# Scores of 64-feature heads over all 128 rows, keys padded with zero halves

## The chip, the cores and the metric

The kernel runs on 1 core of one Trainium2 chip. The metric is the device time of an execution in microseconds (us), as the median of several runs. On the engines' names: TensorE (PE in the rows, with PEld for its weight loads) multiplies matrices, VectorE (DVE) and ScalarE (ACT) work elementwise, POOL (GpSimd) and SP (SyncE) mostly issue transfers and small fills. TensorE multiplies a stationary operand of K rows by up to 128 columns with a moving operand of K rows by N columns; the rows are contracted.

## The reference

256 tokens of 1024 features go through two blocks. The first has FFNs, a pool mixer and multi-head latent attention (MLA) with 16 heads; the second an even layer (forgetting attention and sliding-window attention, 8 heads each, then an FFN) and an odd layer (sparse attention of 16 heads over the 64 best keys that an indexer of 8 heads picks, then a mixture of 8 experts). Cut to the scores:

```python
# MLA: 128 + 64 features
s = einsum('bqhd,bkhd->bhqk', qn_b, k_nope) + einsum('bqhr,bkr->bhqk', qr_b, k_rope)
# even layer: 64 features a head
s = einsum('bqhd,bkhd->bhqk', qi, k) * scale + ci[..., :, None] - cum[..., None, :]   # 8 forgetting heads
s = einsum('bnqhgd,bnshd->bnhgqs', qb, kk) * D ** -0.5                                # 8 window heads, with sinks
# odd layer
logits = einsum('bqhd,bsd->bqhs', iqi, ik)                     # indexer, 8 heads of 64
score = einsum('bqh,bqhs->bqs', iwi, relu(logits))
_, idx = top_k(score, 64)
s = einsum('bqhgd,bqthd->bhgqt', qi, ks) * scale               # 16 heads of 64, over the chosen keys
```

Each is followed by a mask, a softmax over the keys and a product with the values.

## The kernel before

Tokens stand on partitions in two blocks of 128 (`tb`) for the residual stream; operands of a product are transposed, features on partitions. Every float32 operand of a large product is split into a high and a low float32r part: `split` (L157) has ScalarE write the high part (L161, with a factor L164) and VectorE the rest (L162, L166). A product is then three passes, `mm3`, on lines 170, 171 and 172.

`attention` (L745) is a loop over heads, software-pipelined: in turn i it makes the scores of head i and their softmax (`soft`), transposes the weights of head i-2 and splits them (`turn`), and multiplies those of head i-3 with the values (`value`); at the end of a group of heads `project` multiplies with the output weights. In `soft`, the score products fill half of a PSUM tile `psa` per token block; VectorE adds the mask and takes the maximum (L760), ScalarE the exponential with its sum (L764), VectorE one reciprocal for each head (L770), and ScalarE and VectorE one half of the scaling each (L774, L776).

Scores of 64-feature heads use half of the rows: two heads share a tile of 128 partitions, and `score64` (L1002) takes the slice of 64 rows from 0 or from 64 of both operands, `xh` and `xl`, over 256 keys. The MLA's score has a product over 128 rows (`kq`, named `ah`, `al` in the rows) and one over 64, the rotated part, with the shared key `krT` (L986 to 994). `forget` (L1087) adds two products over 64 rows with one column of the constant `sel`. The indexer of the odd layer (L1174) uses `score64` too, eight heads that alternate between the two halves of the rows; its keys lie in a part of `KK`, the tile of the sparse attention's keys.

Operand pairs of 1024 columns come from `xpair`, five buffers. The order of the instructions on each engine is set when the kernel is built: a tile scheduler places them by priority as written and inserts the semaphores; at run time each engine takes its list in order. Loads of one row to all partitions (`brow`, L545) are issued by POOL. Rows of the profile that carry the names `psacc` are products of `project` or of an FFN.

Of the kernel before, what the change touches and what calls it, by code (L numbers as in the profile page):

```python
# [21 lines left out]
P = 128  # L22
# [17 lines left out]
# columns of the constant array  # L40
# [3 lines left out]
def host_consts():  # L44
    """Arrays that depend on shapes alone."""
# [19 lines left out]
    for r in range(8):  # L65
        hc[r::32, C_SEL + r] = 1
# [12 lines left out]
class Net:  # L79
# [49 lines left out]
    def wsplit(self, raw, n):  # L129
        """Splits n <= 1024 columns."""  # L130
        H, L = (self.wp.tile([P, 1024], F32R, tag=t, name=self.nm(t), bufs=6) for t in ("wh", "wl"))
        with self.issued_after(self.hold):
            self.split(H[:, :n], L[:, :n], raw)
        return H[:, :n], L[:, :n]

    def issued_after(self, ins):
        """The work of ins's engine in the block comes after it."""
        return self.tc.issue_after(ins.ins) if ins else nullcontext()

    def wunits(self, w, rows, c0, n, fine=False):  # L140
        """Row blocks of w[:, c0:c0+n], [128, n] each, as a list over k of (H, L)."""
# [15 lines left out]
    def split(self, H, L, src, scale=None):  # L157
        """H + L = src * scale."""
# [20 lines left out]
    def squares(self, x, n, add, scale=1.0):  # L179
        """The sum of (scale * x)^2 over the n features of x [128, n] + add -> [128, 1]."""  # L180
# [13 lines left out]
    def rsqrt(self, v, n):  # L194
        """(v / n)^-1/2: the bits of v give a start, Newton's method the rest."""
# [25 lines left out]
    class XT:  # L221
        """A [1024 features, 256 tokens] operand in two pairs of tiles [128, 4, 256]."""
# [15 lines left out]
    def to_T(self, x, tb, X, g):  # L238
        """X[:, tb] = (x * g)^T."""
# [17 lines left out]
    def xtile(self, tb):  # L257
        return self.xp.tile([P, D], F32, tag=("xh", "xl")[tb], name=self.nm("xn"), bufs=5)

    def normed(self, tb):  # L260
        """rmsnorm without gain."""
# [5 lines left out]
    def normed_twice(self, tb):  # L267
        """h = rmsnorm(h) * gain, then rmsnorm of that without gain."""
# [6 lines left out]
        # with a the mean square of h, b that of t = h * gain: h' = t (a + eps)^-1/2,  # L275
        # h' (b / (a + eps) + eps)^-1/2 = t (b + eps (a + eps))^-1/2
# [6 lines left out]
    def to_T_mod(self, x, tb, X, g, sh):  # L283
        """X[:, tb] = (x * g + sh)^T."""
# [9 lines left out]
    def lin(self, X, w, c0, n, ws=None, feed=None):  # L294
        """Yields (tb, psum) = X^T w[:, c0:c0+n], tokens on partitions; feed(tb) makes X[:, tb]."""
# [14 lines left out]
    def lin_T(self, X, w, c0, n, Q, scale):  # L310
        """Q[H, L] [128, n/128 * 256] = (X^T w[:, c0:c0+n] * scale)^T."""
        for g in range(0, n, 256):
# [7 lines left out]
            self.split(Q[0][:, a:a + 512], Q[1][:, a:a + 512], o, scale)  # L320

    def residual(self, tb, acc, factor, last=True):
        """h[tb] += acc * factor, acc two halves [128, 512]."""
# [6 lines left out]
    def gated_residual(self, tb, acc, g):  # L330
        """h[tb] += acc * g, g [128, 1024] the same on every partition."""
# [19 lines left out]
    def swiglu(self, jobs, hook=None, ws0=None, feed=None):  # L351
        """jobs: (x(k, tb), token blocks, rstd() or None, wg, wu, wd, F, done(tb, acc), which may
        return more to do later); gate and up of a chunk of hidden columns run ahead of the transposes and the down
        product of the one before."""
# [11 lines left out]
        def gate_up(i, up):  # L366
# [3 lines left out]
            # the first chunk takes its token blocks one after the other, as they come  # L370
# [61 lines left out]
        # the last two chunks finish one token block after the other  # L432
# [42 lines left out]
    def then(extra, hook):  # L475
        """A hook that makes one more call in each of its first turns."""
# [16 lines left out]
    def rows(self, rows, vecs):  # L493
        """Vectors of features as rows of 128."""
# [7 lines left out]
    def columns(self, rows, r, at):  # L502
        """The rows as columns."""
# [17 lines left out]
    def constants_late(self):  # L521
# [6 lines left out]
        # rows t' of block b against all tokens: 1 where t' <= token  # L528
# [21 lines left out]
    def ada_plan(self, layer):  # L550
# [21 lines left out]
        def turn(m, acc):  # L572
            """The sum over partitions of acc, as columns."""
# [43 lines left out]
    def gate_rows(self, layer, m):  # L617
        """The gate vector of 1024 features on every partition."""
# [27 lines left out]
        # weights times the scale of their column and the gain of their row  # L646
# [11 lines left out]
        # the first token block needs nothing of the second  # L658
# [26 lines left out]
    def rope(self, src, tab, nh, out):  # L685
        """src, out [128, nh, 64]; tab = (cos, sin) [128, 64] each, both halves alike."""
# [10 lines left out]
    def rope_tables(self):  # L697
        """cos, sin of positions * inv_freq for the second block."""
        nc = self.nc
        pi = self.small(2, I32)  # L700
        nc.gpsimd.dma_start(pi, rowmajor(self.A["positions_2"], (1, P), (P, 2)))
# [4 lines left out]
        # 2 pi in parts whose multiples are exact  # L706
# [26 lines left out]
    def pairs_T(self, x, tb, blocks, Q, base, scale=None):  # L733
        """Q columns base + j*256 + tb*128 = transposed 128-column blocks of x."""
# [3 lines left out]
        H, L = (q[:, base:base + m * S].rearrange("p (j t) -> p j t", j=m)[:, :, tb * P:(tb + 1) * P] for q in Q)  # L738
        self.split(H, L, t[:, :m * P].rearrange("p (j t) -> p j t", j=m), scale)

# [1 line left out]
    # columns of the scores that the queries of a token block can see: [block 0: 128 keys, unused | block 1: 256 keys]  # L742
# [761 lines left out]
```

## Time and profile before

| what | value |
|---|---|
| runs, median (lowest to highest) | 1896.49 us (1894.69 to 1899.66), 3 runs |
| profiled execution, first to last instruction (span) | 1894.1 us; the profile gives no other time for it; the median is 2.4 us above |
| busy: TensorE, VectorE, ScalarE, POOL | 1830.5, 1418.2, 1082.2, 7.0 us |
| mean granted TensorE clock | 0.956 |
| chain that ended last | TensorE 88%, VectorE 7%, ScalarE 3%, DMA 2% |

Reading it: busy time is from the first to the last moment of instructions of an engine, and shares over the whole span mix stages with different limits. The granted clock is the share of TensorE's full speed that the chip lets through; 1.00 is 2.4 GHz and 0.50 is 1.2 GHz. A busy TensorE at 0.50 does half as much.

### The profile page before, as it was taken

How to read it: one execution, taken by the hardware profiler on the slowest of the kernel's cores; microseconds unless marked ns; L12 is line 12 of the kernel's file. 1: busy time of each engine (PE TensorE's matmuls, PEld its weight loads, DVE VectorE, ACT ScalarE, POOL GpSimd, SP SyncE). 2: the span in 40 equal slices, each digit the busy share in tenths (PEclk: the TensorE clock that was granted, in tenths of full speed). 3: DMA queues.
4: the chain of work that ended last, by engine and by line, in shares of the span. 5: the costliest groups of instructions: out<-in, count | busy, mean ns of one | idle time of the engine just before them, and what ended most of it. 6: DMA issues, size and time to landing. Idle time of an engine off the chain costs nothing.

```text
span 1894.1 us, 24484 instructions
## 1 busy us (share of the span) xinstructions
PE 1830.5 (97%) x9045; PEld 1563.8 (83%) x9045; DVE 1418.2 (75%) x2516; ACT 1082.2 (57%) x1704; POOL 7.0 (0%) x21
## 2 busy tenths in 40 slices
PE   8999999999999999999999999999898999999996
PEld 6889788988888888888888878898677888888885
DVE  6668976688767777876775465458936899999997
ACT  6444644465445656544565454356444888777875
POOL 0000000000000000000000000000000000000000
PEclk9999999999999999999997799999858999999998
DMA  8758677767766134776652145555304699999993
GB/s 306 246 195 318 219 278 250 240 222 260 262 216 234 55 123 160 260 259 213 222 167 88 45 137 195 161 190 167 103 15 145 244 337 333 334 331 341 334 359 142
DMA packets 179446, 412.40 MB, mean 218 GB/s; under 512 B 7203, under 2 KB 57574, under 8 KB 179190
## 3 DMA queue, kind: packets, MB, share of 16 engines
q1 hardware_dynamic: 178694, 409.12, 62.4%
q0 software_dynamic: 592, 1.62, 0.3%
q8 instruction: 73, 1.20, 0.3%
q14 instruction: 55, 0.45, 0.1%
q10 hardware_dynamic: 32, 0.01, 0.0%
HBM read 409.67 MB, written 1.05 MB: 217 GB/s over the span
## 4 chain that ended last, share of the span: by engine, by line
PE 88%; DVE 7%; ACT 3%; DMA 2%; issue 1%; SPq 0%; POOL 0%; ACTq 0%; DVEq 0%
PE psa L170 18%; PE psa L171 17%; PE psa L172 17%; PE psacc L170 8%; PE psacc L172 8%; PE psacc L171 8%; PE pstr L236 4%; DVE wl L162 2%; ACT wh L161 1%; PE pstr L171 1%; PE pstr L170 1%; PE psa L1326 1%; PE pstr L172 1%; ACT aa L187 1%; PE pstr L1357 1%
## 5 line engine op out<-in xcount | busy, mean ns | idle before, releaser
L162 DVE TENSOR_TENSOR wl<-raw,wh 128x1024 fp32r<-128x1024 f32 (+2 forms) x720 | 817.2, 1158 | 279.7 <-ACT wh L161 273.5
L161 ACT ACTIVATE wh<-raw 128x1024 fp32r<-128x1024 f32 (+2 forms) x720 | 712.5, 1008 | 514.4 <-PE psa L172 273.9
L170 PE MATMUL psa<-wh,xh 128*128 128x512 f32 (+3 forms) x1536 | 570.2, 372 | 18.4 <-ACT xh L161 11.5
L171 PE MATMUL psa<-wl,xh 128*128 128x512 f32 (+3 forms) x1536 | 564.9, 368 | 3.0 <-DVE wl L162 2.9
L172 PE MATMUL psa<-wh,xl 128*128 128x512 f32 (+3 forms) x1536 | 562.7, 368 | 0.0
L170 PEld LDWEIGHTS psa<-wh,xh 128*128 128x128 f32 x1536 | 290.6, 189 | 60.6 <-ACT xh L161 12.5
L171 PEld LDWEIGHTS psa<-wl,xh 128*128 128x128 f32 x1536 | 290.9, 189 | 42.4 <-DVE wl L162 6.2
L172 PEld LDWEIGHTS psa<-wh,xl 128*128 128x128 f32 x1536 | 290.1, 189 | 37.4 <-DVE xl L166 0.5
L170 PE MATMUL psacc<-wh,ah 128*128 128x512 f32 x616 | 239.7, 393 | 1.5 <-ACT wh L161 1.5
L171 PE MATMUL psacc<-wl,ah 128*128 128x512 f32 x616 | 240.5, 390 | 0.2
L172 PE MATMUL psacc<-wh,al 128*128 128x512 f32 x616 | 240.5, 390 | 0.0
L170 PEld LDWEIGHTS psacc<-wh,ah 128*128 128x128 f32 x616 | 115.6, 188 | 25.1 <-ACT wh L161 2.3
L171 PEld LDWEIGHTS psacc<-wl,ah 128*128 128x128 f32 x616 | 115.8, 188 | 24.3 <-DVE wl L162 1.1
L172 PEld LDWEIGHTS psacc<-wh,al 128*128 128x128 f32 x616 | 115.7, 188 | 24.2
L568 DVE SCALAR_TENSOR_TENSOR big<-raw,csil,big 128x1024 f32<-128x1024 f32 x84 | 107.7, 1282 | 2.7 <-DMA raw<-in_e_ada_w 1.7
L236 PE MATMUL pstr<-ident,aa 128*128 128x128 f32 x432 | 70.5, 293 | 6.5 <-DVE aa L695 5.2
L162 DVE TENSOR_TENSOR al<-pstr,ah 128x512 fp32r<-128x512 f32 (+2 forms) x86 | 52.4, 634 | 29.9 <-ACT ah L161 29.4
L236 PEld LDWEIGHTS pstr<-ident,aa 128*128 128x128 f32 x432 | 54.5, 149 | 17.5 <-issue 3.1
L161 ACT ACTIVATE ah<-pstr 128x512 fp32r<-128x512 f32 (+2 forms) x86 | 44.7, 553 | 25.2 <-PE pstr L236 20.3
L170 PE MATMUL psacc<-wh,xh 128*128 128x512 f32 (+1 forms) x144 | 54.8, 386 | 0.1
L171 PE MATMUL psacc<-wl,xh 128*128 128x512 f32 (+1 forms) x144 | 54.6, 379 | 0.0
L172 PE MATMUL psacc<-wh,xl 128*128 128x512 f32 (+1 forms) x144 | 54.6, 379 | 0.0
(309 smaller groups left out, 1925.3 us busy)
## 6 DMA issues: line engine op xcount, KB each, us to landing
raw<-in_o_exp_down SPq DMA_DIRECT2D x40, 1024.0 KB, 6.7
raw<-in_o_exp_gate SPq DMA_DIRECT2D x32, 1024.0 KB, 8.7
raw<-in_o_exp_up SPq DMA_DIRECT2D x32, 1024.0 KB, 9.7
raw<-in_e_ada_w SPq DMA_DIRECT2D x24, 1024.0 KB, 6.8
raw<-in_o_ada_w SPq DMA_DIRECT2D x24, 1024.0 KB, 5.4
raw<-in_ffn_pre_wd SPq DMA_DIRECT2D x20, 1024.0 KB, 6.4
raw<-in_ffn_post_wd SPq DMA_DIRECT2D x20, 1024.0 KB, 6.3
raw<-in_ffn_pre_wu SPq DMA_DIRECT2D x16, 1024.0 KB, 5.7
```

What stands on the lines that cost most here:

```text
L161: nc.scalar.activation(H, src, AF.Copy)
L162: nc.vector.tensor_sub(L, src, H.bitcast(F32))
L170: mm(out, x[0], w[0], start=start, stop=False)
L171: mm(out, x[0], w[1], start=False, stop=False)
L172: mm(out, x[1], w[0], start=False, stop=stop)
L187: nc.scalar.activation(junk[:, c], x[:, c], AF.Square, scale=scale, accum_out=ss[:, i:i + 1])
L236: self.nc.tensor.transpose(out[:, j * P:(j + 1) * P], src[:, b * P:(b + 1) * P], self.ident)
L568: nc.vector.scalar_tensor_tensor(acc, src, self.csil[:, k:k + 1], acc, op0=ALU.mult, op1=ALU.add)
L1326: nc.tensor.matmul(o[:, j * S:(j + 1) * S], XN[tb][part][:, (k + j) * P:(k + j + 1) * P], sel[tb], start=n == 0, stop=n == 3)
L1357: nc.tensor.matmul(t, selT[e][:, tb * P:(tb + 1) * P], y[hf][part], start=part == 0, stop=part == 1)
```

## The change

Keys of the 64-feature heads get 128 rows: each head pair's keys are written twice as wide, into two blocks of 256 columns, of which the first has keys on rows 0 to 63 and zeros below, and the second zeros above and keys on rows 64 to 127. The query operand is not altered: it holds two heads on its 128 rows, and the zeros cancel the other head. So every score product of `score64`, of the MLA's rotated part and of `forget` contracts 128 rows, with the same number of columns. The zeros are written by POOL (`zero_pads`), and the split of the keys goes in two halves of 64 partitions (`pad_split`). The indexer's keys get their own pair `IK`. Keys of the even layer's forgetting heads now take two pairs `K`, so `xpair` has a sixth buffer; its space comes from a smaller ring for DMA descriptors (`dynamic_dma_scratch_size=1024`), and the row loads of `brow`, the positions and the router's weights are issued by ScalarE's queue, not by POOL.

```diff
     def xpair(self):
-        return self.pair("x", 1024, 5)
+        return self.pair("x", 1024, 6)
...
-        hc[r::32, C_SEL + r] = 1
+        hc[r:64:32, C_SEL + r] = 1
...
+    def zero_pads(self, K):
+        for t in K:
+            for half in range(2):
+                v = t.rearrange("p (b x t) -> p b x t", x=2, t=S)[64 - half * 64:128 - half * 64, :, half, :]
+                self.nc.gpsimd.memset(v.bitcast(F32), 0.0)
+        return K
+
+    def pad_split(self, K, b0, src, toks):
+        m = src.shape[1]
+        for half in range(2):
+            r = slice(half * 64, half * 64 + 64)
+            H, L = (t.rearrange("p (b x t) -> p b x t", x=2, t=S)[r, b0:b0 + m, half, toks] for t in K)
+            self.split(H, L, src[r])
...
     def brow(self, dst, src, n):
-        self.nc.gpsimd.dma_start(dst, rowmajor(src, (0, P), (1, n)))
+        self.nc.scalar.dma_start(dst, rowmajor(src, (0, P), (1, n)))
...
-        self.cT, self.krT = self.pair("cT", S, 1), self.pair("krT", S, 1)
+        self.cT, self.krT = self.pair("cT", S, 1), self.zero_pads(self.pair("krT", 2 * S, 1))
...
-                self.mm3(o, self.sl(qr, slice(b, b + 64), slice(c, c + P)), self.sl(self.krT, slice(b, b + 64)), False, True)
+                self.mm3(o, self.sl(qr, slice(None), slice(c, c + P)), self.sl(self.krT, slice(None), slice(k, k + S)), False, True)
...
-    def score64(self, Q, qb, K, kb, base, extra=None):
+    def score64(self, Q, qb, K, b, half, extra=None):
+        k = slice((2 * b + half) * S, (2 * b + half + 1) * S)
         def f(tb, o):
-            r = slice(base, base + 64)
-            self.mm3(o, self.sl(Q, r, slice(qb + tb * P, qb + (tb + 1) * P)), self.sl(K, r, slice(kb, kb + S)),
+            self.mm3(o, self.sl(Q, slice(None), slice(qb + tb * P, qb + (tb + 1) * P)), self.sl(K, slice(None), k),
                      True, extra is None)
...
-        Q, K = self.xpair(), self.xpair()
+        Q, K = self.xpair(), [self.zero_pads(self.xpair()) for _ in range(2)]
...
-                b = slice(hd % 2 * 64, hd % 2 * 64 + 64)
-                e1 = sel[b, hd:hd + 1]
-                nc.tensor.matmul(o, e1.to_broadcast([64, P]), ck[b, :S], start=False, stop=False)
-                nc.tensor.matmul(o, cq[b, tb * P:(tb + 1) * P], e1.to_broadcast([64, S]), start=False, stop=True)
+                e1 = sel[:, hd:hd + 1]
+                nc.tensor.matmul(o, e1.to_broadcast([P, P]), ck[:, :S], start=False, stop=False)
+                nc.tensor.matmul(o, cq[:, tb * P:(tb + 1) * P], e1.to_broadcast([P, S]), start=False, stop=True)
...
-        IQ, KK = self.xpair(), self.xpair()
+        IQ, IK, KK = self.xpair(), self.zero_pads(self.pair()), self.zero_pads(self.xpair())
...
-    nc = _bacc.Bacc("TRN2", target_bir_lowering=False, num_devices=1)
+    nc = _bacc.Bacc("TRN2", target_bir_lowering=False, num_devices=1, dynamic_dma_scratch_size=1024)
```

`lin_T` and `pairs_T` get an argument `padded`, by which they call `pad_split` in place of `split`; the keys of the forgetting and window heads, of the indexer and of the sparse attention are made with it.

Three places of the built order. First ScalarE in the even layer, before: `ah` from `pstr` is the window heads' keys K2, `xh` from `psa` the forgetting heads' keys K (a number names a buffer's instance).

```order
L164 ACTIVATE xh_8884<-pstr_9257 128x4x128
L161 ACTIVATE ah_8882<-pstr_9264 128x128
L164 ACTIVATE xh_8884<-pstr_9268 128x4x128
L161 ACTIVATE ah_8882<-pstr_9275 128x128
L161 ACTIVATE wh_9430<-raw_9428 128x1024
L161 ACTIVATE wh_9434<-raw_9428 128x1024
L161 ACTIVATE xh_9133<-psa_9289 128x512
L161 ACTIVATE wh_10054<-raw_10052 128x1024
L161 ACTIVATE wh_10058<-raw_10052 128x1024
L161 ACTIVATE xh_9133<-psa_9350 128x512
```

And now:

```order
L164 ACTIVATE xh_8894<-pstr_9277 128x4x128
L161 ACTIVATE ah_8888<-pstr_9284 64x128
L164 ACTIVATE xh_8894<-pstr_9290 128x4x128
L161 ACTIVATE ah_8888<-pstr_9297 64x128
L161 ACTIVATE ah_8888<-pstr_9284 64x128
L161 ACTIVATE ah_8888<-pstr_9297 64x128
L161 ACTIVATE wh_9458<-raw_9456 128x1024
L161 ACTIVATE wh_9462<-raw_9456 128x1024
L161 ACTIVATE xh_9143<-psa_9313 64x2x256 x2
L161 ACTIVATE wh_10082<-raw_10080 128x1024
L161 ACTIVATE wh_10086<-raw_10080 128x1024
L161 ACTIVATE xh_9149<-psa_9376 64x2x256 x2
```

The key splits have doubled in number, over 64 partitions each; the weight splits (`wh`) and the query splits around them stand where they stood. VectorE's list, not shown, goes the same way with the low parts.

Second VectorE in the odd layer, ahead of the indexer: `xl` of four blocks is the indexer's queries, `xl` 128x128 its keys, `wl` weights, L692 to 695 the rotation of the sparse attention's keys. Before:

```order
L162 TENSOR_TENSOR Vl<-psa_12033,Vh 128x4x64
L162 TENSOR_TENSOR xl_11817<-pstr_12097,xh_11816 128x128
L162 TENSOR_TENSOR xl_11815<-pstr_12101,xh_11814 128x4x128
L162 TENSOR_TENSOR xl_11817<-pstr_12108,xh_11816 128x128
L162 TENSOR_TENSOR wl_12367<-raw_12360,wh_12366 128x1024
L162 TENSOR_TENSOR wl_12449<-raw_12446,wh_12448 128x1024
L692 TENSOR_TENSOR sg_12173<-psa_12122,tab_7972 128x256
L693 TENSOR_TENSOR aa_12174<-psa_12122,tab_7973 128x256
```

And now, with the keys in `al`:

```order
L162 TENSOR_TENSOR Vl<-psa_12070,Vh 128x4x64
L162 TENSOR_TENSOR Vl<-psa_12071,Vh 128x4x64
L162 TENSOR_TENSOR al_11845<-pstr_12135,ah_11844 64x128
L162 TENSOR_TENSOR xl_11843<-pstr_12141,xh_11842 128x4x128
L162 TENSOR_TENSOR al_11845<-pstr_12135,ah_11844 64x128
L162 TENSOR_TENSOR al_11845<-pstr_12148,ah_11844 64x128
L162 TENSOR_TENSOR wl_12413<-raw_12406,wh_12412 128x1024
L162 TENSOR_TENSOR al_11845<-pstr_12148,ah_11844 64x128
L162 TENSOR_TENSOR wl_12495<-raw_12492,wh_12494 128x1024
L712 TENSOR_TENSOR sg_12215<-psa_12164,tab_7978 128x256
L713 TENSOR_TENSOR aa_12216<-psa_12164,tab_7979 128x256
```

Four rows stand in place of two, between the indexer's query splits and the weights. The keys of the sparse attention, `xl` 128x2x128, go from two rows to four in the same way, among the rows of the indexer's sums.

Third POOL's list around the even layer, before:

```order
L1014 MEMSET sg_7720 128x512
L547 DMA big_8575<-in_final_norm 128x1024
L547 DMA sm_8880<-in_e_forget_b 128x8
L547 DMA sm_9496<-in_e_sinks 128x8
L1246 MEMSET sm_13373 128x8
L547 DMA sm_13274<-in_o_router_b 128x8
L547 DMA gb<-in_final_norm 128x1024
```

And now:

```order
L1038 MEMSET sg_7726 128x512
L331 MEMSET ah_8888 64x256 x2
L331 MEMSET al_8889 64x256 x2
L331 MEMSET xh_9143 64x2x256 x2
L331 MEMSET xh_9149 64x2x256 x2
L331 MEMSET xl_9144 64x2x256 x2
L331 MEMSET xl_9150 64x2x256 x2
L1270 MEMSET sm_13419 128x8
```

The row loads have left for ScalarE's list, where each stands behind the work that was written ahead of it (the last, of `gb`, behind the last head's weights of the odd layer), and fills of the key tiles have come. TensorE's list has as many rows as before, 10458, and the same order but for a few transposes and for the operands' names.

## Rows read from the trace of the kernel before

**Rows 1.** The page, slices: busy tenths of TensorE, its granted clock.
```profile
PE   8999999999999999999999999999898999999996
PEclk9999999999999999999997799999858999999998
```

**Rows 2.** Windows: stretch, us, busy of PE, PEld, DVE, ACT, POOL, then PEclk.
```profile
660.00:680.00 20.00, 20.00 (x141) 17.39 (x140) 15.86 (x48) 13.48 (x40) 0.00 (x0) 1.00 0.16 54
1014.20:1065.30 51.10, 51.10 (x198) 42.95 (x197) 24.33 (x100) 24.09 (x88) 0.00 (x0) 0.50 0.04 14
1372.60:1420.30 47.70, 47.70 (x166) 37.24 (x165) 18.89 (x79) 19.64 (x68) 0.00 (x0) 0.50 0.05 20
```

**Rows 3.** Windows at the edges of the low clock, same columns.
```profile
1010.70:1014.00 3.30, 1.25 (x10) 0.93 (x9) 1.89 (x9) 3.04 (x11) 0.00 (x0) 1.00 0.41 89
1065.40:1068.70 3.30, 3.30 (x15) 3.04 (x14) 1.48 (x7) 2.14 (x8) 0.00 (x0) 0.50 0.00 0
1068.80:1072.20 3.40, 3.35 (x20) 2.92 (x20) 1.96 (x7) 3.40 (x13) 0.00 (x0) 1.00 0.00 0
1356.00:1358.80 2.80, 1.24 (x6) 0.64 (x5) 1.81 (x6) 0.96 (x2) 0.00 (x0) 1.00 0.52 203
1362.00:1372.60 10.60, 9.34 (x38) 7.73 (x36) 8.20 (x27) 6.82 (x23) 0.00 (x0) 0.50 0.41 113
1468.10:1471.50 3.40, 3.40 (x18) 3.40 (x18) 0.96 (x7) 1.39 (x4) 0.00 (x0) 0.50 0.03 5
1471.60:1475.00 3.40, 3.40 (x26) 3.18 (x25) 1.91 (x6) 3.40 (x8) 0.00 (x0) 1.00 0.00 0
```

**Rows 4.** Groups of TensorE, 1065.4 to 1068.7: shapes, count, busy us, mean ns.
```profile
L171 PE MATMUL pstr<-pT1l,Vh 128*128 128x256 f32 x2 | 1.0, 498 | 0.0
...
```

**Rows 5.** Groups of TensorE, 1468.1 to 1471.5, same columns.
```profile
L1326 PE MATMUL psa<-sel,xh 128*128 128x256 f32 x9 | 3.9, 434 | 0.7 <-DVE sel L1320 0.7
...
```

**Rows 6.** Timeline of TensorE in the MLA: start us, duration us, line, operation.
```profile
660.49 0.28 PE L172 MATMUL psa<-ah,al 128*128 128x256 f32 x1
660.70 0.38 PE L170 MATMUL psa<-krTh,xh 64*128 64x256 f32 x1
660.92 0.28 PE L171 MATMUL psa<-krTl,xh 64*128 64x256 f32 x1
661.04 0.28 PE L172 MATMUL psa<-krTh,xl 64*128 64x256 f32 x1
```

**Rows 7.** Tile krTh on TensorE: duration ns, first and last start.
```profile
L170 PE MATMUL psa<-krTh,xh x32: 380/383/387, 634.4 to 724.0; 64*128 64x256 f32 x32
```

**Rows 8.** Timeline of TensorE in the even layer's attention.
```profile
1041.37 0.41 PE L171 MATMUL psa<-al,xh 64*128 64x256 f32 x1
1041.59 0.41 PE L172 MATMUL psa<-ah,xl 64*128 64x256 f32 x1
1041.93 0.69 PE L236 MATMUL pstr<-ident,aa 128*128 128x128 f32 x2
```

**Rows 9.** Windows of line 770 alone, one reciprocal per head.
```profile
1012.10:1070.50 58.40, 2.62 (x16) 0.53 0.06 19
1363.20:1423.40 60.20, 2.57 (x16) 0.50 0.11 36
```

**Rows 10.** Groups of VectorE, 1315 to 1345: key splits.
```profile
L162 DVE TENSOR_TENSOR xl<-pstr,xh 128x256 fp32r<-128x256 f32 x2 | 0.8, 419 | 0.0
...
L162 DVE TENSOR_TENSOR xl<-pstr,xh 128x128 fp32r<-128x128 f32 x2 | 0.6, 282 | 0.0
```

**Rows 11.** Windows ahead of the two attention stages.
```profile
980.00:1000.00 20.00, 20.00 (x154) 19.35 (x153) 11.86 (x19) 9.32 (x14) 0.00 (x0) 1.00 0.57 186
1328.00:1340.00 12.00, 11.30 (x50) 9.01 (x50) 11.91 (x52) 6.86 (x11) 0.00 (x0) 1.00 0.27 89
```

**Rows 12.** Groups of TensorE in the indexer, 1323.7 to 1327.2.
```profile
L170 PE MATMUL psa<-xh,xh 64*128 64x256 f32 x16 | 2.8, 293 | 0.0
...
```

**Rows 13.** Timeline of POOL: a row load's issue, idle time before.
```profile
1439.32 0.53 POOL L547 DMA_DIRECT2D gb<-in_final_norm  x1 [470.83 <-PE pstr L172]
```

More of the change, by code (lines that the diff above doesn't have):

```diff
@@ L308, in order, with lin_T @@
         return [(k, tb) for k in range(nk) for tb in range(ntb)]
-    def lin_T(self, X, w, c0, n, Q, scale):
+    def lin_T(self, X, w, c0, n, Q, scale, padded=False):
         for g in range(0, n, 256):
@@ L319, in lin_T @@
             a = g // P * S
-            self.split(Q[0][:, a:a + 512], Q[1][:, a:a + 512], o, scale)
+            if padded:
+                self.pad_split(Q, a // S, o.rearrange("p (b t) -> p b t", b=2), slice(None))
+            else:
+                self.split(Q[0][:, a:a + 512], Q[1][:, a:a + 512], o, scale)
+    def zero_pads(self, K):
[10 more added lines that the diff above has]
+            self.split(H, L, src[r])
     def residual(self, tb, acc, factor, last=True):
@@ L731, in rope_tables, with pairs_T @@
                 nc.vector.tensor_copy(t[:, 32:64], t[:, 0:32])
-    def pairs_T(self, x, tb, blocks, Q, base, scale=None):
+    def pairs_T(self, x, tb, blocks, Q, base, scale=None, padded=False):
         t = self.psum("tr")
@@ L737, in pairs_T @@
         self.transposes(t, x, blocks)
-        H, L = (q[:, base:base + m * S].rearrange("p (j t) -> p j t", j=m)[:, :, tb * P:(tb + 1) * P] for q in Q)
-        self.split(H, L, t[:, :m * P].rearrange("p (j t) -> p j t", j=m), scale)
+        src, toks = t[:, :m * P].rearrange("p (j t) -> p j t", j=m), slice(tb * P, (tb + 1) * P)
+        if padded:
+            return self.pad_split(Q, base, src, toks)
+        H, L = (q[:, base:base + m * S].rearrange("p (j t) -> p j t", j=m)[:, :, toks] for q in Q)
+        self.split(H, L, src, scale)
     KEYS = (slice(0, P), slice(S, 2 * S))
@@ L892, in mla_kv_finish @@
         self.split(*self.cT, tc_[:, :S], self.gcol("ckv_norm", 0, 1))
-        self.split(*self.krT, tk[:, :S])
+        self.pad_split(self.krT, 0, tk[:, None, :S], slice(None))
     def mla(self, h):
@@ L1032, in even_mix @@
         self.brow(fb, A["e_forget_b_2"], 8)
-        K2, Q2 = self.pair(), self.xpair()
+        K2, Q2 = self.zero_pads(self.pair()), self.xpair()
         z = self.small(16)
@@ L1064, in even_mix @@
             self.pairs_T(xq[tb], tb, range(4), Q2, 0, 0.125)
-            self.pairs_T(xk[tb], tb, (0,), K2, 0)
-        self.lin_T(X, w, 512, 512, K, None)
+            self.pairs_T(xk[tb], tb, (0,), K2, 0, padded=True)
+        for g in range(2):
+            self.lin_T(X, w, 512 + g * 256, 256, K[g], None, padded=True)
         cum = self.psum("tr")
@@ L1100, in even_mix @@
         for hd in range(8):
-            heads.append((None, self.score64(Q, hd // 2 * S, K, hd // 2 * S, hd % 2 * 64, forget(hd)), self.mask,
+            heads.append((None, self.score64(Q, hd // 2 * S, K[hd // 4], hd // 2 % 2, hd % 2, forget(hd)), self.mask,
                           self.vslot(hd), None, hd // 2, hd % 2 == 0, hd % 2 == 1))
         for hd in range(8):
-            heads.append((window_values if hd == 1 else None, self.score64(Q2, hd % 4 * S, K2, 0, hd // 4 * 64), self.swa_mask,
+            heads.append((window_values if hd == 1 else None, self.score64(Q2, hd % 4 * S, K2, 0, hd // 4), self.swa_mask,
                           self.vslot(hd // 4 * 2 + hd % 2), (sinks[:, hd:hd + 1], nsinks[:, hd:hd + 1]), 4 + hd // 2, hd % 2 == 0, hd % 2 == 1))
@@ L1165, in odd_mix @@
             self.pairs_T(xq[tb], tb, range(4), IQ, 0)
-            self.pairs_T(xk[tb], tb, (0,), KK, 512)
+            self.pairs_T(xk[tb], tb, (0,), IK, 0, padded=True)
         keys = []
@@ L1183, in odd_mix @@
         for tb in range(NT):
-            self.pairs_T(keys[tb], tb, range(2), KK, 0)
+            self.pairs_T(keys[tb], tb, range(2), KK, 0, padded=True)
         cur = list(score)
@@ L1216, in odd_mix @@
             kv = hd // 4
-            heads.append(((lambda: turn_queries(1)) if hd == 3 else None, self.score64(Q[hd // 8], hd % 4 * S, KK, hd // 8 * S, kv % 2 * 64), masks,
+            heads.append(((lambda: turn_queries(1)) if hd == 3 else None, self.score64(Q[hd // 8], hd % 4 * S, KK, hd // 8, kv % 2), masks,
                           self.vslot(2 * kv + hd % 2), None, hd // 2, hd % 2 == 0, hd % 2 == 1))
```

11 lines of the change are left out of this document (5 added, 6 removed).

## The prediction

> **What bounds the kernel now.** I read the page first: TensorE's line reads 9 in nearly each of the 40 slices of some 47 us, but the granted clock reads 7 in slices 22 and 23, and 8, 5 and 8 in slices 29 to 31 [rows 1]. So the question is what TensorE does there, not who it waits for. The second view was busy time by windows of one stage each [rows 2]: in 660 to 680 us (MLA) TensorE is busy 20.00 of 20 us and does 141 matmuls at clock 1.00; in the attention of the even layer it is busy 51.10 of 51.10 us, does only 198, at 0.50, and in that of the odd layer 47.70 of 47.70 us with 166, at 0.50. 0.50 is the 1.2 GHz level, 1.00 the 2.4 GHz level. VectorE and ScalarE are busy less than half of those two stretches, 24.33 and 24.09 us, and 18.89 and 19.64 us, so TensorE at half clock is the bound there.
>
> The third view was the edges of the low stretches, in windows [rows 3]. Both begin where TensorE has just been idle: it is busy 1.25 of 3.30 us from 1010.7 and 1.24 of 2.80 us from 1356.0. That they begin is thus explained; that they last is not, since TensorE is full from then on. Before the clock comes back TensorE did this: from 1065.40 to 1068.70 it ran nothing but value products and transposes, all of 128 rows (seven groups, the first of them in [rows 4]), and right after, from 1068.80, the clock is 1.00. The score products of 64 rows had just ended. The odd layer's end reads alike. In all the stretch before, scores of 64 rows are mixed with the rest. MLA, which has scores of 64 rows too, but on top of as many of 128, stays at 1.00. I read this as: after work in which scores of 64 rows have this share the granted clock does not rise, and after work over 128 rows it does.
>
> The last views were two timelines of TensorE. At full clock two matmuls alike, of 256 columns, start 0.12 us apart; where 128 rows change to 64 or back the step is 0.21 to 0.22 [rows 6]. At half clock the step is 0.22 and at a change 0.34 [rows 8].
>
> **The change part by part.**
> *Clock in the two attention stages.* The columns that TensorE streams do not change (256 per score matmul over 128 or 64 rows), so its need at full clock is the count by the spacing of [rows 6]: even 198 x 0.12 = 23.8 us, odd 166 x 0.12 = 19.9 us. The other engines' work is the same per head: 24.3 us VectorE and 24.1 us ScalarE even, 18.9 and 19.6 us odd [rows 2]. So even is bound by three nearly equal loads, at least 24.3 us; with the scraps lost where three engines take turns it can be as much as 24.3 / 0.79 = 30.7 us, 0.79 being VectorE's share in the MLA window, where TensorE is full. I take 27.5, the middle: 51.1 - 27.5 = -23.6 (-20.4 to -26.8). Odd: at least 19.9, by the same share 25.2 us; I take 22.5: -25.2 (-22.5 to -27.8). The ends, 3.3 us each at half clock [rows 3], halve: -1.65 each. The beginnings: the idle time ahead of them stays, so the clock falls as before, and some time passes until it is back. For the even layer I put in two stretches of 3.3 us, which do the work of 3.3 us: +3.3. For the odd layer the 10.6 us from 1362.0 at 0.50 [rows 3] are kept as they are: 0. Even -22.0, odd -26.9, together **-48.9 us**. Reciprocals, one per head, check this: 16 stand in 58.4 us even and 60.2 us odd [rows 9], 3.65 and 3.76 us a head; the sum says 2.3 and 2.1.
>
> *Changes of row count in the MLA.* On the way into the 64-row part the first start is 0.09 us late and the next 0.10 [rows 6]; the way back I take to cost from half of that to as much again, so 0.28 to 0.38 us for an excursion, and there are 32 (32 such matmuls between 634.4 and 724.0) [rows 7]: 9 to 12 us. TensorE is full there, VectorE at 0.79 and ScalarE at 0.67 [rows 2], so most of it should come off: **-8 us** (0, if another engine's order sets the pace, to -12).
>
> *Extra splits.* A padded key operand is split in two halves of 64 partitions, with the same columns, so each split becomes two of about the same time. 128 columns take VectorE 0.28 us and 256 take 0.42 [rows 10], so 512 some 0.70; ScalarE is about as fast. Even layer: two more of 512 columns and two of 128 on either engine, 2.0 us, beside a TensorE that is the bound (20.00 of 20 us busy from 980, ScalarE 9.32, VectorE 11.86 [rows 11]): 0, and 2.0 if that cover were gone. Odd layer: from 1328 to 1340 VectorE is busy 11.91 of 12 us [rows 11] and the top-64 selection that follows has to finish before the scores can be masked. There the indexer's keys add two of 0.28 us and the keys of the sparse attention two of 0.42 us to VectorE, +1.4 us, all on the path.
>
> *The indexer's lost pairing.* Its 48 matmuls over 64 rows alternate between the two halves of the rows and ran in 3.4 us (16 on each of three lines) [rows 12], 0.07 apart, closer than the 0.12 of [rows 6]: pairs run side by side. With 128 rows they need 48 x 0.12 = 5.8 us, 2.4 more; VectorE has other work in part of it: +1.1 (0 to 2.4). Together the odd layer's chain costs **+2.5 us** (1.4 to 3.8). The page "TensorE: Matmul & The Clock Gate" of the Trainium skill, section "Why this matters for your kernels", says that matmuls with few rows run concurrently if they lie in distinct row groups, and so speaks against padding; the indexer's row bears it out, the attention's does not, since there the six matmuls of a head sit in the same half and start 0.22 us apart as those of 128 rows do. By that rule alone the sum would take the 2.4 and no gain.
>
> *Row loads moved to ScalarE's queue.* Nine DMA issues leave POOL, 0.53 us for the one shown [rows 13], some 5 us in all; ScalarE has room in the stretches of [rows 2] and [rows 11], and the two at its start stand ahead of work that waits for the first input anyway. Three of them are rows of 1024 features that wait for a buffer (the one shown waited 470.83 us on POOL); on ScalarE such a wait would hold up the weight splits behind it. The order puts them late, behind work that has waited for the same engine, so 0, at worst +3 for all (a few us of splits late, which the six weight buffers cover). POOL's 20 new memsets cost nothing: it stands idle for hundreds of us at a time [rows 13], and the tiles that they clear are asked for before the stages' products begin.
>
> *Sixth operand buffer.* It lets one more operand pair be filled ahead. In the experts, the last ten slices, TensorE's line reads 9 throughout but for the end [rows 1], so there is nothing to win: 0 (0 to -2).
>
> Sum: -48.9 - 8 + 2.5 = **-54.4 us**. The profiled execution spans 1894.1 us; the runs' median is 1896.5, 2.4 above it, which I keep: 1894.1 - 54.4 + 2.4 = **1842.1 us**. With the parts' bounds mostly independent I put 1826 to 1856 for this case.
>
> **The rivals.**
> *A, the clock rises, but the heads run at the pace of their chains.* A head's chain goes TensorE, VectorE, ScalarE, VectorE, ScalarE, TensorE, with few buffers, and three loads are nearly equal. If a head takes 2.7 us, 16 x 2.7 = 43.2 us in place of 58.4 and 60.2: -15.2 - 17.0 - 8 + 2.5 = -37.7, **1859 us**. If idle moments let the clock drop again for some time, as after 1010.7, it ends here or up to 1868. For it: the even layer's loads within 2%. Against: MLA's heads go through the same chain with the same buffers, and TensorE is full there.
>
> *B, the clock stays low.* It may be that padding with zeros does not count, or that transposes and VectorE's pace keep it down. Then only the changes of row count go. Of the even stretch 198 x 0.22 = 43.6 us is plain steps and 7.5 us is not, of the odd one 36.5 and 11.2; of that I take 7 and 9, so -16 - 8 + 2.5 = -21.5, **1875 us**. For it: TensorE was full and yet at half clock. Against: the ends of both stretches, and 1468.10 to 1471.50, where only products with a one-hot operand ran (two groups of nine, one shown) [rows 5], mostly zeros, and the clock was 1.00 right after [rows 3]. The page "TensorE: Matmul & The Clock Gate" of the Trainium skill, in "Part 1: The HAM clock gate", says that the gate follows how busy TensorE has been; taken as the trace's busy time, which was full already, that gives B, and the rows of the low stretches speak against taking it so.
>
> *C, slower: TensorE gets idle moments in the MLA and its clock falls there.* Today's MLA is full because the changes of row count fill it. Without them it waits for VectorE (0.79 of the time) at each head; both long low stretches began after idle time of that sort. If the full clock is lost for 30 of the MLA's 90 us (634 to 724) these take up to 60, +30 us, and with attention left at half clock: +30 - 16 + 2.5 = +16.5, **1913 us**. [...] Against: VectorE's lead is 4 us in 20, in small pieces.
>
> *D, no effect that can be measured:* the clock stays low and the saved steps turn into waiting for the odd layer's VectorE chain, about 1896 us.
>
> **How the numbers follow.** Forecast 66%, A 17%, B 8%, C 5%, D 4%. A difference under 0.3% (5.7 us) can't be told from no change. Faster by more: forecast, A and B, 0.91; within: D, 0.04; slower: C, 0.05. The range has to hold 8 in 10: the forecast's own 1826 to 1856 and A up to its late end, 1826 to 1868.
>
> **What would show it.** The windows of the two attention stretches should show clock 1.00 except in the first 3 to 7 us, and 16 reciprocals in some 35 us each. The score rows should read 128*128, and no step in the MLA's score timeline should exceed 0.12 us but for the transposes. The indexer should take 5 to 6 us. VectorE's busy time from the indexer to the masks should be 1.4 us longer. POOL should hold only memsets. If the clock reads 0.50 for most of either stretch, my reading of the clock is wrong; if it reads 1.00 and a head takes over 2.6 us, the error is in how I let three equal loads overlap.

## The result and the profile after

The changed kernel takes 1832.39 us (median of 4 runs, 1830.92 to 1833.26), the kernel before 1897.49 us (1894.69 to 1899.66): ratio 0.9655, 95% interval 0.9641 to 0.9668. That is -65.1 us where -54.4 was forecast; the time lies in the range. The profiled execution spans 1830.6 us in place of 1894.1, and its mean granted clock is 0.983 in place of 0.956.

First the slices of the page of the changed kernel, as in [rows 1]:

```profile
PE   8999999999999999999989989999898999999996
PEclk9999999999999999999999999999997999999999
```

The two dips of the clock in the attention stages are gone. What is left is one slice at 7: a low stretch from 1389.0 to 1409.5, ahead of the experts, where the kernel before was low too (1454.5 to 1471.5). Then windows of the changed kernel, with the columns of [rows 2]: the MLA, the time ahead of the even layer's attention, that attention, the time around the first heads of the odd layer's, and that attention:

```profile
640.00:660.00 20.00, 20.00 (x171) 20.00 (x170) 17.82 (x57) 17.12 (x50) 0.00 (x0) 1.00 0.16 54
1000.40:1003.70 3.30, 1.75 (x16) 1.59 (x15) 1.89 (x9) 3.04 (x11) 0.00 (x0) 1.00 0.38 81
1004.00:1030.00 26.00, 24.87 (x203) 23.67 (x202) 22.05 (x100) 24.09 (x89) 0.00 (x0) 1.00 0.07 27
1327.60:1334.30 6.70, 5.57 (x25) 5.30 (x25) 5.37 (x18) 4.96 (x13) 0.00 (x0) 0.50 0.37 105
1338.00:1358.00 20.00, 19.96 (x169) 19.76 (x170) 17.75 (x84) 19.92 (x72) 0.00 (x0) 1.00 0.17 55
```

Against [rows 2] the even stage does 203 matmuls in 26.0 us, not 198 in 51.1, and the odd one 169 in 20 us, not 166 in 47.7, both at 1.00. ScalarE is now busy 24.09 of 26.00 and 19.92 of 20.00 us, TensorE 24.87 and 19.96: both are nearly full. The second row is the idle time ahead of the even layer's attention, the same place as 1010.70 in [rows 3]: TensorE is busy 1.75 of 3.30 us there, not 1.25, and the clock did not fall after it. In the odd layer it fell at 1327.5 (fourth row) and was back at 1334.4.

Line 793 is the reciprocal that was line 770; its windows in the MLA, the even and the odd stage, to set beside [rows 9] (columns: stretch, us, VectorE busy with the count, clock, DMA):

```profile
641.70:719.40 77.70, 2.61 (x16) 1.00 0.34 116
1001.80:1033.70 31.90, 2.58 (x16) 1.00 0.11 34
1330.40:1360.40 30.00, 2.59 (x16) 0.93 0.23 71
```

Sixteen heads in 31.9 and 30.0 us, in place of 58.4 and 60.2. Next TensorE's timeline in the MLA (start, duration), to set beside [rows 6]:

```profile
650.38 0.28 PE L172 MATMUL psa<-ah,al 128*128 128x256 f32 x1
650.50 0.28 PE L170 MATMUL psa<-krTh,xh 128*128 128x256 f32 x1
650.62 0.28 PE L171 MATMUL psa<-krTl,xh 128*128 128x256 f32 x1
650.74 0.28 PE L172 MATMUL psa<-krTh,xl 128*128 128x256 f32 x1
650.86 0.28 PE L170 MATMUL psa<-ah 128*128 128x256 f32 x1
```

The late starts have gone: from 128 rows of `ah` to `krTh` and back each start is 0.12 us after the last. Last the indexer's first pass, on the tile of its keys (durations min/median/max in ns, first and last start):

```profile
L170 PE MATMUL psa<-ah,xh x16: 283/283/283, 1287.7 to 1293.1; 128*128 128x256 f32 x16
L172 PE MATMUL psa<-ah,xl x16: 283/283/283, 1288.0 to 1293.4; 128*128 128x256 f32 x16
```

Its products, of 128 rows now, take 5.7 us from the first start to the last; in the kernel before, the 48 of [rows 12] took 3.2.

Where the time went can be read off ScalarE's weight splits, 720 in both kernels in the same order. These are the starts of some of them in the two profiled executions, and by how much the difference changed since the line above:

```
split  stage that has just ended        before us  after us  difference  step
217    first block ahead of the MLA         605.5     608.3        +2.8  +2.8
253    MLA                                  761.8     753.3        -8.5 -11.3
337    even layer, ahead of attention       994.6     984.4       -10.2  -1.7
361    even attention                      1134.7    1097.4       -37.4 -27.2
438    odd layer, ahead of attention       1355.4    1322.8       -32.6  +4.8
439    odd attention                       1427.0    1363.2       -63.8 -31.2
709    experts                             1855.9    1792.6       -63.3  +0.5
```

### The profile page after: what moved, and what is told of

It is laid out like the page before. It is cut to its first block, busy times and chain, and to the rows that moved or that the text cites. A ratio compares the mean times of both kernels' runs of the same rounds, so it can differ in the third digit from the quotient of the medians.

```text
span 1830.6 us, 24518 instructions
## 1 busy us (share of the span) xinstructions
PE 1765.8 (96%) x9045; PEld 1526.3 (83%) x9045; DVE 1417.7 (77%) x2525; ACT 1084.7 (59%) x1713; POOL 11.8 (1%) x37
## 4 chain that ended last, share of the span: by engine, by line
PE 85%; DVE 7%; ACT 4%; DMA 2%; issue 1%; SPq 0%; ACTq 0%; DVEq 0%
PE psa L170 18%; PE psa L171 17%; PE psa L172 17%; PE psacc L170 9%; PE psacc L172 8%; PE psacc L171 8%; PE pstr L236 3%; DVE wl L162 2%; ACT wh L161 1%; PE psa L1350 1%; PE pstr L1381 1%; ACT sg L787 1%; DMA raw<-in_ffn_pre_wg 0%; ACT aa L187 0%; DMA raw<-in_ffn_pre_wd 0%
## 5 line engine op out<-in xcount | busy, mean ns | idle before, releaser
L162 DVE TENSOR_TENSOR al<-pstr,ah 128x512 fp32r<-128x512 f32 (+2 forms) x92 | 54.2, 612 | 31.9 <-ACT ah L161 31.3
L236 PE MATMUL pstr<-ident,aa 128*128 128x128 f32 x432 | 64.3, 275 | 8.8 <-DVE aa L715 6.5
```

The costliest lines, as they stand in the source:

```text
L162: nc.vector.tensor_sub(L, src, H.bitcast(F32))
L236: self.nc.tensor.transpose(out[:, j * P:(j + 1) * P], src[:, b * P:(b + 1) * P], self.ident)
```

## The experiments

All start from the changed kernel. Where a run takes back rows, it takes back the rows alone: the tiles stay padded, and a product reads 64 of their 128 rows (`r` below). So the fills, the doubled splits and the buffers are the same. Runs given as one run are to be set beside the changed kernel's nine, 1830.92 to 1837.42 us.

```diff
-            self.mm3(o, self.sl(Q, slice(None), q), self.sl(K, slice(None), k), True, extra is None)
+            r = slice(half * 64, half * 64 + 64) if rows == 64 else slice(None)
+            self.mm3(o, self.sl(Q, r, q), self.sl(K, r, k), True, extra is None)
```

**e1_all64: all scores back to 64 rows.** `rows=64` everywhere, in the MLA and in `forget` too.

> The changed kernel with every padded score read over its 64 live rows alone (MLA's rotated part, forgetting, window, indexer, sparse attention); the doubled splits, the fills, the sixth buffer and the moved row loads stay. Theory R (the rows that a score contracts decide the clock): all of the gain goes, both attention stages at 0.50 and 16 reciprocals in 58 and 60 us; 1895 to 1900 us, 1.4 of it for the doubled splits. Rival (buffers and moved loads bring part of the gain): under 1890 us, with landmarks ahead of the MLA earlier than in the kernel before.

Measured: 1900.56 us (10 runs), a little above the expected 1900, ratio to the kernel before 1.0013 (0.9987 to 1.0039). The reciprocals of the two stages:

```profile
1014.20:1072.60 58.40, 2.63 (x16) 0.53 0.06 19
1368.00:1428.40 60.40, 2.48 (x16) 0.50 0.11 35
```

58.4 and 60.4 us, at 0.53 and 0.50, as in [rows 9] (58.4 and 60.2). So the buffer, the moved loads, the fills and the splits bring nothing that the runs can tell from no change; the gain hangs on the rows. The landmarks ahead of the MLA were 2.2 us later than in the kernel before, not earlier.

**e2_dsa64: 64 rows in the sparse attention alone.**

> The changed kernel with 64 rows in the scores of the odd layer's sparse attention alone. Theory R: the clock is 0.50 in that stage and only there, 16 reciprocals in about 60 us in place of 30; 1832 + 29 = 1861 us; the even layer's stage stays at 32 us. Rival (once the clock is up at the stage's start it stays, whatever the rows): 1832 to 1840 us, clock 1.00.

Measured: 1863.83 us (one run). Windows of the even and the odd stage:

```profile
1004.00:1030.00 26.00, 25.07 (x204) 24.10 (x205) 21.55 (x98) 24.09 (x89) 0.00 (x0) 1.00 0.12 41
1340.00:1390.00 50.00, 50.00 (x176) 39.17 (x176) 20.34 (x86) 20.44 (x72) 0.00 (x0) 0.50 0.06 21
```

The even stage is as in the changed kernel, the odd one as in the kernel before: 0.50 to its end, though the clock fell at the same point as in the changed kernel (1327.0, there 1327.5). The loss of 31 us stays in its stage.

**e3_dsa_switch: 128 rows, with changes of row count.** The rival is that the late starts at each change of row count are what holds the clock down.

```diff
+            self.nc.tensor.matmul(o[:, :16], Q[0][0:64, q], K[0][0:64, k.start:k.start + 16], start=True, stop=True)
             self.mm3(o, self.sl(Q, slice(None), q), self.sl(K, slice(None), k), True, extra is None)
```

> The changed kernel, with a product of 64 rows and 16 columns ahead of each of the 32 score groups of the sparse attention, whose result is overwritten. TensorE changes its row count 64 times in the stage, as the kernel before did, but the scores contract 128 rows. Theory R: the clock stays at 1.00 and the stage is longer by 32 x (0.19 + 0.05) = 8 us at most, so 1833 to 1841 us. Rival S (the stalls at changes of row count keep the clock down, not the rows): clock 0.50, 16 reciprocals in over 50 us, over 1852 us.

Measured: 1847.45 us (one run). TensorE's timeline first, then the windows before and after the clock came back:

```profile
1355.85 0.27 PE L1031 MATMUL psa<-xh,xh 64*128 64x16 f32 x1
1356.06 0.39 PE L170 MATMUL psa<-xh,xh 128*128 128x256 f32 x1
1356.28 0.28 PE L171 MATMUL psa<-xl,xh 128*128 128x256 f32 x1
1356.40 0.28 PE L172 MATMUL psa<-xh,xl 128*128 128x256 f32 x1
1356.60 0.27 PE L1031 MATMUL psa<-xh,xh 64*128 64x16 f32 x1
```

```profile
1328.00:1348.00 20.00, 18.89 (x69) 15.79 (x69) 11.75 (x45) 9.56 (x30) 0.00 (x0) 0.50 0.32 106
1350.00:1370.00 20.00, 20.00 (x136) 17.52 (x135) 13.28 (x57) 14.28 (x49) 0.00 (x0) 1.00 0.00 1
```

Each small product makes three starts late, of 0.20 to 0.22 us in place of 0.12: its own and those of the two products behind it. That is 0.39 us more for a group, where the expectation had 0.24. The clock was 0.50 from 1327.7 to 1348.2, some 14 us longer than in the changed kernel, and then 1.00 to the end of the stage. So neither forecast held: the return came later, which the theory did not say (1841 at most), but it came, and the rival's 0.50 and over 1852 us are refuted. Whether the late starts or the small 64-row products as such delay the return is not separated.

**e4_dsa64_fill: 64 rows, and as many products over 128 rows.** The same 64-row scores as in the second run, with three full products ahead of each group, overwritten by them.

```diff
+            self.mm3(o, self.sl(Q, slice(None), q), self.sl(K, slice(None), k), True, True)
+            r = slice(half * 64, half * 64 + 64)
             self.mm3(o, self.sl(Q, r, q), self.sl(K, r, k), True, extra is None)
```

> Scores of the sparse attention over 64 rows as in the second run, but ahead of each score group the same three products over all 128 rows, whose result is overwritten: 96 more matmuls of 256 columns. Theory R, with the share of 64-row work at 6 of 21 matmuls a head in place of 6 of 15 (MLA before had it at about a fifth and kept 1.00): the clock is 1.00, a head needs 18 x 0.12 + 0.3 + 4 x 0.1 = 2.9 us, 16 heads 46 us, about 1848 us, so faster than the second run though it does more. Rival S, or an activity that the added work doesn't raise: clock 0.50 and 96 x 0.213 = 20 us on top of the second run, 1881 us.

Measured: 1861.01 us (one run), windows before and after the clock's return:

```profile
1330.00:1356.00 26.00, 26.00 (x91) 20.62 (x91) 10.78 (x41) 8.93 (x31) 0.00 (x0) 0.50 0.26 82
1357.00:1387.00 30.00, 30.00 (x199) 25.02 (x200) 17.38 (x68) 18.28 (x62) 0.00 (x0) 1.00 0.00 1
```

The clock came back at 1356.2, after 27 us, and a head then took 3.2 us. The direction is the theory's (96 matmuls more, and 3 us less, though by single runs), the size was not: the clock was to be 1.00 and a head 2.9 us, and the late return and 0.3 us a head ate 13 us of the forecast gain.

**e8_dsa_half: 64 rows in every second head.** `rows=64 if hd % 2 else 128`.

> The changed kernel with 64 rows in the scores of every second head of the sparse attention, 128 in the others, so 3 of 15 matmuls a head on average are of 64 rows. Theory R by share (MLA kept 1.00 with about a fifth of its matmuls over 64 rows, the attention stages fell with two fifths): the clock returns within some us of the stage's start, as in the changed kernel or somewhat later, 16 reciprocals in 32 to 38 us, 1834 to 1840 us. Rival (any 64-row scores in this loop hold it down): clock 0.50 throughout, over 1855 us.

Measured: 1843.35 us (one run):

```profile
1331.50:1345.00 13.50, 11.23 (x46) 9.76 (x47) 10.71 (x39) 8.56 (x26) 0.00 (x0) 0.50 0.40 122
1345.10:1371.00 25.90, 25.85 (x180) 22.29 (x180) 19.10 (x84) 21.99 (x77) 0.00 (x0) 1.00 0.05 18
```

The clock was back 13.6 us after its fall, where the changed kernel took 6.8; the stage's 16 reciprocals took 36.5 us, as expected. The total is 3 us over the bound, which went by a changed kernel of 1832 us: on this run's chip that took 1836.71 (e6 below), 6.6 less than this run, and 6.5 of it lies in this stage.

**e9_dsa64_pair: 64 rows, the other 64 at work beside them.** Each 64-row product is followed by one over the other half, with the keys' zeros, into a tile that nobody reads.

```diff
+                for i, (a, c) in enumerate(((0, 0), (0, 1), (1, 0))):
+                    self.nc.tensor.matmul(o, Q[a][r, q], K[c][r, k], start=i == 0, stop=i == 2)
+                    self.nc.tensor.matmul(d[:, :S], Q[a][e, q], K[c][e, k], start=i == 0, stop=i == 2)
```

> Scores of the sparse attention over 64 rows as in the second run, but each of the 6 products of a head is followed by one over the other 64 rows (the zero half of the keys, result not used), so that the two can run side by side as in the indexer: twice as many 64-row matmuls, and all 128 rows at work. Theory R (rows at work decide): the clock returns to 1.00 within 7 to 20 us of the stage's start, 16 reciprocals in 32 to 45 us, 1834 to 1850 us, faster than the second run (1864). Rival M (matmuls of 64 rows as such, or the changes to and from them, hold the clock down): 0.50 throughout, 16 reciprocals in 55 us or more, 1858 us or more.

Measured: 1836.38 us (one run). The timeline of one group (L1038 is the score, L1039 its companion), and the windows at the stage's start and within:

```profile
1345.17 0.38 PE L1038 MATMUL psa<-xh,xh 64*128 64x256 f32 x1
1345.18 0.38 PE L1039 MATMUL psacc<-xh,xh 64*128 64x256 f32 x1
1345.40 0.28 PE L1038 MATMUL psa<-xl,xh 64*128 64x256 f32 x1
1345.40 0.28 PE L1039 MATMUL psacc<-xl,xh 64*128 64x256 f32 x1
1345.52 0.28 PE L1038 MATMUL psa<-xh,xl 64*128 64x256 f32 x1
1345.52 0.28 PE L1039 MATMUL psacc<-xh,xl 64*128 64x256 f32 x1
```

```profile
1327.10:1333.80 6.70, 5.64 (x39) 4.79 (x41) 5.70 (x17) 4.78 (x13) 0.00 (x0) 0.50 0.38 110
1340.00:1360.00 20.00, 19.87 (x194) 17.09 (x192) 15.04 (x66) 16.44 (x57) 0.00 (x0) 1.00 0.07 26
```

The pairs start 0.00 to 0.01 us apart, and the clock came back as early as in the changed kernel (at 1333.8, 6.8 us after its fall), although every score is a 64-row matmul and the late start behind the first of a group (0.22) is still there. This is the run that decides: what the stage lacked was rows at work, not 128-row instructions, and not freedom from late starts. It is one trace, but the three with 64-row scores in all heads and nothing added (before, e1, e2) stayed low for 64.8 to 64.9 us. The companions' keys are all zeros, so zeros count; how they compare with data no run shows.

**e7_mla64: 64 rows in the MLA's rotated part alone.**

> The changed kernel with the rotated part of the MLA's scores over its 64 live rows. Theory D (what the MLA gained are the late starts at changes of row count, 0.28 to 0.38 us for each of 32 excursions, at full clock): clock 1.00 throughout the MLA, reciprocals over 88 us in place of 77.4, 1842 to 1844 us. Rival (part of the MLA's gain is clock): a stretch at 0.50 between 640 and 730 us, over 1846 us. Rival (VectorE sets the MLA's pace): under 1838 us.

Measured: 1845.20 us (one run); its reciprocals in the MLA:

```profile
641.60:729.90 88.30, 2.60 (x16) 1.00 0.30 102
```

88.3 us at 1.00 in place of 77.7 at 1.00: 10.6 us for 32 excursions, 0.33 us each, and no clock in it. The total is 1.2 us above the expected range, on the chip where the changed kernel took 1836.71.

**e5_idx64, e6_after_again, e11_idx64_again: the indexer back to 64 rows.** `rows=64` in the indexer alone.

> The changed kernel with the indexer's scores over their 64 live rows, so that heads alternate between the two halves of the rows again; all else as changed. Theory P (the indexer lost its pairing): its 48 matmuls take 3.4 us in place of 5.8 and the odd layer's chain ahead of the attention is 1 to 2.4 us shorter, 1830 to 1831.5 us. Rival (VectorE sets the pace there, the pairing is hidden): no difference over 0.5 us at the landmarks. Rival (64-row work, even little, lets the clock fall there for longer): slower by 2 us or more.

> The changed kernel once more, for comparison on the same chip with the run above: 1832 us, ratio 0.9655 to the kernel before.

> The version of the fifth run once more, to stand beside the run above: 1831 to 1835 us, and the indexer's stretch again some 2 us shorter than in the changed kernel.

Measured on one chip: 1832.03 us (1831.76 to 1835.12) against 1836.71 (1833.20 to 1837.42) for the changed kernel, 5 runs each; ratios to the kernel before 0.9653 (0.9636 to 0.9670) and 0.9670 (0.9652 to 0.9687), which overlap. The later run gave 1833.87 (0.9674, 0.9636 to 0.9711). The tile of the keys in the fifth run:

```profile
L170 PE MATMUL psa<-ah,xh x16: 275/280/383, 1287.8 to 1290.8; 64*128 64x256 f32 x16
L172 PE MATMUL psa<-ah,xl x16: 274/278/282, 1288.2 to 1291.0; 64*128 64x256 f32 x16
```

3.2 us from the first to the last start, where the changed kernel has 5.7. But little of that reaches the work behind: from weight split 425, ahead of the indexer, to 433, behind it, the traces have 28.9 us in e1, e5 and e11 and 29.5 in both of the changed kernel. So the pairing is worth 0.6 us here, close to the rival that it is hidden and below the 1 to 2.4 expected. The fifth run's trace gains 1.5 us more ahead of the indexer, where it has no low stretch like the changed kernel's at 1259.3 to 1262.7; the later run, the same kernel, has one, so that is not the rows' doing. The medians agree in sign but their intervals don't separate the versions. Two medians lie above what was expected: 1832.03 (1830 to 1831.5), and 1836.71 for the changed kernel (1832), whose ratio of 0.9670 has the expected 0.9655 within its interval.

**e10_idx64_pool: part of ScalarE's work to POOL.**

```diff
-                    nc.scalar.activation(sm[:, c], sm[:, c], AF.Copy, scale=ri[:, tb:tb + 1])
+                    nc.gpsimd.tensor_scalar(sm[:, c], sm[:, c], ri[:, tb:tb + 1], None, op0=ALU.mult)
```

> The version of the fifth run, with the scaling of the first token block's softmax (L797, 0.39 us a head on ScalarE) done by POOL, in all three attention stages. Theory: in the even and odd stages ScalarE now sets the pace (19.92 of 20 us busy from 1338); without 0.39 us of 1.98 a head, heads need 1.7 to 1.9 us: 3 to 6 us less, 1826 to 1829 us. Rival (POOL takes 0.8 us or more for 128 columns and the head's chain or VectorE gets slower): 1835 us or more.

Measured: 1838.23 us (1837.44 to 1839.58), 4 us over the run beside it (e11, 1831.14 to 1836.00); the ratios' intervals overlap (0.9661 to 0.9733), but each of its four runs is above each of the four there. That is the rival's side (1835 or more), not the theory's (1826 to 1829). The groups of POOL between 1335 and 1360:

```profile
L797 POOL TENSOR_SCALAR sg<-sg,sm 128x128 f32<-128x128 f32 x6 | 4.4, 735 | 90.0 <-DVE sm L793 88.8 <-PE psa L172 1.2
L797 POOL TENSOR_SCALAR aa<-aa,sm 128x128 f32<-128x128 f32 x6 | 4.1, 691 | 8.1 <-DVE sm L793 8.1
```

0.69 to 0.74 us on POOL in place of 0.39 on ScalarE, inside each head's chain. The heads got no shorter: 16 reciprocals of the even stage span 2.2 us more than in e11 (33.9 in place of 31.7 from the first start to the last), those of the odd stage 0.4 less (30.4, 30.8). Lifting ScalarE's load alone, in this way, gains nothing.

## Why the prediction came out as it did

*The clock, the main term, was right in cause and too small.* Forecast -48.9 us for the two stages; by the splits -27.2 and -31.2, together -58.4. The reading of [rows 3] and [rows 4] held, and the runs narrow it: in the odd layer's stage the clock was low for 6.8 us after its fall in the changed kernel, 6.8 with pairs, 13.6 with half the heads at 64 rows, 20.5 with a small 64-row product ahead of each group, 27.4 with added full products, and to the end with 64 rows alone. All but the first and the last are single traces; in six traces with plain 128-row scores it was 6.8, in two of them with 3.4 more after a short return.

Three sizes were off. The head was put at 2.3 and 2.1 us and takes 2.0 and 1.9 (31.9 and 30.0 us for 16): three nearly equal loads overlapped better than the 0.79 of the MLA's VectorE suggested (0.93 for ScalarE in the even stage). For the odd layer the low start was kept as long as before, up to 1372.6, 13.7 us after the fall; it lasted 6.8. And +3.3 us for a low start of the even stage was not paid: the clock did not fall there. The prediction had said that the idle time ahead stays and the clock falls as before. But that time got shorter too (TensorE busy 1.75 of 3.30 us, not 1.25). Both traces with 64-row scores in the even stage fell (before, e1), none of the eleven with 128 rows did; whether the rows behind the idle time or its length made the difference is not shown.

*The MLA*: -8 forecast, -11.3 measured by the splits, and the run that takes it back loses the same 11.3 between them (10.6 by the reciprocals). The bound of 9 to 12 us was right; the discount for other engines was not needed. The Trainium skill, "TensorEngine Tiling (Array Packing)", section "Key Properties", says that changing the tiling mode drains TensorE. The traces agree for the start at the change, 0.21 us beside 0.12 without one [rows 6]. The start after it, between two products of 64 rows, is as late (0.22), which that sentence does not cover.

*The odd layer's chain*: +2.5 forecast, +4.8 measured. 1.5 of it lies ahead of the indexer, in the low stretch at 1259.3 to 1262.7, which came and went between traces of one kernel (e5, e11). From split 425 to 433, across the indexer, the kernel before took 28.3 us, the versions with 64 rows there 28.9 and the changed kernel 29.5: 0.6 for the lost pairing, where 1.1 was put in, and 0.6 for the rest of the padding, although VectorE's doubled split rows cost the 1.4 us that were forecast (1.42). The other 2.1 us gather between split 433 and 438. The clock was low there for 6.8 us (1313.9 to 1320.7), in the kernel before for 3.4; four traces with a 128-row indexer and a low stretch of 3.4 (e2, e3, e4, e7) reach split 438 1.2 to 1.5 us earlier than the changed kernel's, counted from split 425. What remains is not separated. So more than half of the 4.8 us comes with stretches at the low clock, which the prediction had not put into this term.

*Moved loads and buffers*: forecast 0. Nothing was gained, but +2.8 us had gathered by 605 us, and e1 had +2.2 there. 1.0 came in the first 30 us, where the clock rose at 13.4 us rather than 10.6, and the rest around 185 to 216 us, where a weight split waited 3.2 us for its load in place of 0.6. Whether the moved issues cause either was not tried; the eleven other traces with moved loads were 1.3 to 4.5 us late at 605 us. The prediction counts nine issues and 20 fills; the traces have eight and 24, which changes no term. The -1.7 us ahead of the even layer's attention was in no term either; that stretch takes 231.5 to 233.5 us in the other traces, 232.8 in the kernel before and 231.1 in the changed one, so it is within the scatter.

*The rivals.* B (the clock stays low, zeros not counted) is refuted by the result and by e9. A was wrong in its 2.7 us a head. C, idle moments in the MLA: TensorE stayed full there (20.00 of 20 us) at 1.00. B's page, "TensorE: Matmul & The Clock Gate" of the Trainium skill, "Part 1: The HAM clock gate", ties the clock to how busy TensorE is. The trace's busy share is not the measure of that: e2 stayed at 0.50 while TensorE was busy 50.00 of 50.00 us, and in e9 the clock rose out of a stretch with 5.64 of 6.70.

Nor is the row count by itself. Ahead of the experts the kernel before has a stretch at 0.50 in which TensorE is busy throughout with products of 128 rows, 18 of 19 of them only 8 columns wide (the window, with the columns of [rows 2], and its largest group):

```profile
1461.50:1465.00 3.50, 3.50 (x19) 3.50 (x17) 1.29 (x7) 1.54 (x4) 0.00 (x0) 0.50 0.01 2
L1241 PE MATMUL psa<-sm,aa 128*128 128x8 f32 x14 | 3.1, 352 | 0.0
```

The clock was back only at 1471.5, after some idle time and then the products of 256 columns of [rows 5]. What the runs show of rows holds for products of 256 columns; what exactly the clock follows stays open.

## What to carry to other kernels

Look at the granted clock by stage, not at the mean: a stage that is full on TensorE and still at 1.2 GHz may be worth up to half its length (here 58.4 and 60.2 us became 31.9 and 30.0). If its matmuls contract 64 rows, fill the other rows, with zeros (padding the operand) or with another 64-row product beside. Padding cost TensorE nothing here: at full clock a product of 256 columns starts 0.12 us after the last, over 64 rows [rows 6] as over 128. Leave it off where 64-row products of both halves already run side by side, as in the indexer (48 products in 3.2 us, padded 5.7), though only 0.6 us of that reached the work behind.

## What was not expected of the hardware

Zeros in half of the moving operand's rows are enough for the full clock: 1.00 in both stages of the changed kernel, but for the first 6.8 us of the odd one; a version with data in all rows was not run. A run of three 64-row products between 128-row ones costs 0.33 us at full clock (10.6 us for 32). And the kernel before is not always equally slow: 2 of its 33 runs took 1884.15 and 1886.33 us with mean clocks of 0.963 and 0.964, the others 1893.88 to 1901.82; of e1's ten runs one took 1883.08 with 0.966. There is no trace of these three, so where their clock came back earlier stays open.
